# One transformer layer on one core: FFN's first weight block by halves of the tokens in the passage, a later copy in the shift, dot products in other heads, new operand offsets

## The chip, the cores and the metric

The kernel runs on one core of a Trainium2 chip. The metric is the device time of one execution in microseconds (us). A profile of one execution is read with it; its times count from the start of its span.

## The reference

One layer of a diffusion transformer for 256 latent tokens and 256 context tokens, width D = 2048, all in fp32:

```python
h = modulate(rms_norm(x, g_attn_pre), sh1, sc1)          # latent tokens
hc = modulate(rms_norm(ctx, g_attn_pre), csh1, csc1)     # context tokens
# window attention (8 heads, 2 key heads, rotary, sinks) and
# neighbourhood attention (8 heads, position bias), both with the context as further keys
y = (sigmoid(ga) * (oa @ w_br_a) + sigmoid(gb) * (ob @ w_br_b)) @ w_o
x = x + gt1 * rms_norm(y, g_attn_post)
h = modulate(rms_norm(x, g_ffn_pre), sh2, sc2)
a, g = split(depthwise_conv(h @ w_up, conv_w, conv_b))   # conv over tokens, width 3
x = x + gt2 * rms_norm((silu(g) * a) @ w_down, g_ffn_post)
```

The six modulation vectors come from `silu(c) @ w_mod + b_mod`. `w_up` is 2048 x 11264, `w_down` 5632 x 2048.

## The kernel before

Every fp32 product is made of fp32r matmuls on TensorE (PE): each operand is split into a high part (ScalarE, ACT, copies it as fp32r) and a low part (VectorE, DVE, subtracts). `split` at L123 does both; L127 is ACT's copy, L131 DVE's subtraction. A product is high x high, high x low and low x high. In `mm2` the first two are one matmul of 512 columns (the moving operand holds the high and low parts of 256 tokens side by side) and the third is one of 256 columns.

Weights come as blocks of 128 x 2048 in the order of use: `raw_block` loads one over SyncE's DMA queue (SP), `halves` splits it in two pieces of 128 x 1024, `block(ahead)` hands out the next block, splits the one after it and loads `ahead` blocks further. `place` names other memory for a block's split, `queue` instructions behind which it has to stand.

The stages: keys with the modulation vectors (`dot`, `mods`), where `shift` is part of the last keys; values; 16 attention heads with the query projections as filler in between; gates and branches; W_O (`norm_gain`, matmuls `py_o`); the passage to the FFN; `w_up` in blocks (`pu`); `w_down` (`py_d`). A Tile scheduler puts each engine's instructions in order; where the program says `tc.issue_after(i)` an instruction stands behind `i`, and under `manual_schedule` PE's order is that of the code.

The parts that the change touches:

- **The passage.** `norm_gain` runs W_O in four chunks `c` of 512 output columns over two token halves `t` (128 tokens each). In the last chunk the last `lead` = 2 weight blocks are run for t = 0 first, then for t = 1, twelve matmuls a block and half, so that t = 0 is closed earlier. `close(t)` squares on ACT (`Square`, row sums in `ss`) and multiplies by the gain on DVE (`yg`); `residual(t)` (`done`) adds to the stream (`x1`, STT of DVE, L988) and takes the sums of squares of the result; `rstd_tok` gives 1/rms in `r`. For t = 1 the last 512 columns of the residual are made by PE itself (`ident` x `x1`, then the diagonal `dg` x `yg`), to save DVE's steps. The normalised result goes to FFN's layout by transposes on PE into `ptx`: `turn(b, ts)` transposes group b of 128-column tiles j; `scaled(t, c0, c1)` multiplies tiles c0 to c1 by `r` ahead of it (into `yg`); for t = 0 and the first four groups the diagonal `dg1` does that on PE. `split_h2(b)` makes high and low parts of h: ACT L1043 (with scale and shift), DVE L1047 and L1048; every fourth tile by ACT L1042 and L1043 and DVE L1045. `first_pairs(k)` runs the four output tiles `pu0..3` for tile k of the contraction. `keep_busy` runs matmuls of no use while PE would wait (L236).
- **Shift.** The last of the six vectors' products with PE (`pmsh`), copied by ACT (`evsh`, L567), and transposed back.
- **Attention.** Per head: `scores` (`s`), softmax on ACT and DVE, `transposes` (`pT`), `values` (`po`); `q_rope` rotates the queries of the window heads. Every operand lies in one tile `room` at offsets counted in T2 = 512. Four `mods` dot products on DVE stand behind heads p = 1, 4, 7, 10.

PSUM has six banks of `acc` and two of `bank`.

Of the kernel before, what the change touches and what calls it, by code (L numbers as in the profile page):

```python
# [15 lines left out]
P = 128  # L16
# [42 lines left out]
def layer_kernel(ctx, tc, xc, xt, ccol, crow, wm_sc, wm_sd, wm_sh, wm_b, cols, wk, wkt, ws, rope, mask_a, bias_b, out):  # L59
# [74 lines left out]
    def halves(r, off, pool=None, after=None):  # L134
        n = r.shape[-1]
        b = 1 if pool else 2
        h, lo = (
            (pool or wp).tile([P, 2048 + 128], F32R, tag=f"w{q}", bufs=b, name=f"w{q}{nraw[0]}")[:, off : off + 2048]
            for q in "hl")
        for q in (slice(0, n // 2), slice(n // 2, n)):  # L140
            last[:] = split(h[:, q], lo[:, q], r[:, q], after)
        return h, lo
# [98 lines left out]
    with ExitStack() as mx:  # L241
# [10 lines left out]
        with ExitStack() as at:  # L252
# [279 lines left out]
            for k in range(KT):  # L532
# [27 lines left out]
                for i in range(k % 4 == 1, NK2):  # L560
                    keys(pk[i], *units[KT + k // 2], (k % 2) * NK2 * P + i * P, k)
                    if k == KT - 2 and i < 2:
# [4 lines left out]
                        nc.scalar.activation(ev[:, :n_], pm[:, 2 * P * i : 2 * P * i + n_], AF.Copy)  # L567
# [122 lines left out]
            def q_split(hd, t):  # L690
                o = 4 * T2 + order.index(hd) % 3 * T2
# [42 lines left out]
            def keys_of(hd):  # L734
                i = NHB + hd // GRP if hd < NHA else hd - NHA
                if i not in ks:
                    o = [(len(ks) % 2 * 2 + q) * T2 for q in range(2)]
                    ks[i] = [room[:, q : q + T2] for q in o]
                    split(*ks[i], kT[:, i], last)
                return ks[i]  # L740

            def vals_of(hd):
                i = hd // GRP if hd < NHA else 2 + hd - NHA
                if i not in vs:

                    o = [(12 + len(vs) % 2 * 2 + q) * T2 - 8 for q in range(2)]
# [32 lines left out]
            def transposes(hd):  # L779
                pT = pTs[hd] = room[:, 7 * T2 : 11 * T2].rearrange("p (b a s) -> p b a s", b=4, a=2)  # L780
# [25 lines left out]
            for p in range(NH + 1):  # L806
# [14 lines left out]
                if p in (1, 4, 7, 10):  # L821
# [48 lines left out]
    def norm_gain(act, nk, yg, grow, ss, nm, lead, done, extra=None):  # L870


        for c in range(4):
            py = [acc(f"py_{nm}{c}_{t}") for t in range(2)]
# [13 lines left out]
            def close(t, after=None):  # L888
                with ExitStack() as es:
                    if after:  # L890
                        es.enter_context(tc.issue_after(after))
                    nc.scalar.activation(yg[:, t, cs], py[t][:], AF.Square, accum_out=ss[:, t, c : c + 1])
                nc.vector.tensor_tensor(out=yg[:, t, cs], in0=py[t][:], in1=grow[:, cs], op=ALU.mult)
# [13 lines left out]
            else:  # L907
# [4 lines left out]
                for t in range(2):  # L912
                    if t:
                        for i, g in enumerate(range(n - lead, n)):
                            part(wts[i], g, 1)
                    close(t, after)
                    after = done(t)
# [14 lines left out]
    with ExitStack() as ys:  # L932
# [20 lines left out]
        crb = silu_row(yp)  # L953
        gain_row(0, grow)
        place[b0 + B_UP - 1] = yp

        pu, dg = [], {}

        def diagonal(n, t):

            dg[n] = yp.tile([P, P], F32, name=f"dg{n}")
            return nc.scalar.activation(dg[n][:], ident[:], AF.Copy, scale=r[:, n, t : t + 1]).ins
# [7 lines left out]

        def residual(t):
            rstd_tok(ss[:, 0, t], r[:, 0, t : t + 1])
            c3 = slice(1536, 2048)
            if t:

                pu.extend(acc(f"pu0_{i}") for i in range(4))
                px = pu[3]
                with tc.issue_after(final[0]):
                    p_ = nc.tensor.matmul(px[:], ident[:], x1[:, t, c3], start=True, stop=False).ins
                with tc.issue_after(p_):  # L980
                    b_ = keep_busy(4, "2", pu[0])
                with tc.issue_after(diagonal(0, t)):
                    diagonal(1, 0)
                with tc.issue_after(b_):
                    p_ = nc.tensor.matmul(px[:], dg[0][:], yg[:, t, c3], start=False, stop=True).ins
            for c in range(3 if t else 4):
# [5 lines left out]
                if t and c == 2:  # L992
# [9 lines left out]
            if t == 0:  # L1002
                rstd_tok(ss[:, 1, t], r[:, 1, t : t + 1])
                return a_.ins
            with tc.issue_after(v_.ins), tc.issue_after(a_.ins):
                return p_, rstd_tok(ss[:, 1, t], r[:, 1, t : t + 1])[0]

        p_, q_ = norm_gain(zz, KT, yg, grow, ss[:, 0], "o", 2, residual, beside)
        zs.close()


        group = [(0,)] + [(j, j + 1) for j in range(1, KT - 1, 2)] + [(KT - 1,)]
        ptx, behind = {}, []

        def turn(b, ts, js=None):

            if b not in ptx:
                ptx[b] = (acc if b % 2 else bank)(f"ptx{b}")
            for t in ts:
                for f, j in enumerate(group[b]):  # L1020
                    if js and j not in js:
                        continue
                    d = ptx[b][:, f * S + t * P : f * S + t * P + P]
                    if t == 0 and b < 4:
                        nc.tensor.matmul(d, x1[:, t, j * P : j * P + P], dg[1][:], start=True, stop=True)
                    else:
                        nc.tensor.transpose(d, yg[:, t, j * P : j * P + P], ident[:])

        def split_h2(b):
            with ExitStack() as es:  # L1030
                for i_ in behind:
                    es.enter_context(tc.issue_after(i_))
                behind[:] = split_tiles(b)
            return behind

        def split_tiles(b):
            for f, j in enumerate(group[b]):
                g_, s_ = gcol[:, 1, j : j + 1], modx[:, 16 + j : 17 + j]
                px = ptx[b][:, f * S : f * S + S]
                t_ = up.tile([P, S], F32, tag="half", bufs=2, name=f"h2t{j}")  # L1040
                if j % 4 == 3:
# [273 lines left out]
```

## Time and profile before

| | |
|---|---|
| median of 3 runs | 1512.99 us (1512.9 to 1513.67) |
| the profiled execution | 1512.95 us, span 1511.0 us |
| PE busy | 1499.6 us, 99% |
| DVE busy | 1132.4 us, 75% |
| ACT busy | 781.6 us, 52% |
| TensorE clock granted | 0.999 |

A row of the trace in order of time has start and duration in us, the engine, the line of the code, the operation, `out<-in` with shapes, and in brackets the idle time of the engine ahead of it and what ended that. `x4` joins four instructions. A plain fp32 matmul leaves two records. "PE A <- B" in a list of waits is time in which PE stood for B: total, times, longest. Of the chain that ended last, PE has 97%.

### The profile page before, as it was taken

What the parts mean: (1) busy time and instruction counts of PE and PEld (TensorE: products, weight loads), DVE (VectorE), ACT (ScalarE), POOL (GpSimd) and SP (SyncE); (2) the same over time, 40 slices, a digit from 0 to 9 for tenths busy, and PEclk for the clock granted to TensorE, in tenths of its full rate; (3) what the DMA queues carried; (4) which work ended last, traced back from release to release, by engine and by line L of the source; (5) the groups of instructions that cost most, each with busy time, mean ns of one, the idle gap of its engine ahead of it and who ended that gap; (6) DMA issues with size and microseconds to landing.
All of it is one profiled execution on the core that took longest, in us unless ns stands there. A gap on an engine that the chain in (4) does not pass through costs nothing.

```text
span 1511.0 us, 21644 instructions
## 1 busy us (share of the span) xinstructions
PE 1499.6 (99%) x8549; PEld 1289.3 (85%) x8549; DVE 1132.4 (75%) x1679; ACT 781.6 (52%) x1277; POOL 1.6 (0%) x10
## 2 busy tenths in 40 slices
PE   9999999999999999999999999999999999999998
PEld 7876889898888888888888888888888888888886
DVE  4496997999988888877678888788788776444444
ACT  4342542777764455554467555555555555344342
POOL 0000000000000000000000000000000000000000
PEclk9999999999999999999999999999999999999999
DMA  9988779754368888879846676666666556555552
GB/s 368 401 319 335 273 290 341 263 168 168 140 252 294 324 327 308 309 268 356 309 178 226 249 250 220 238 243 236 234 248 232 192 192 257 217 195 195 195 195 84
DMA packets 59253, 381.07 MB, mean 252 GB/s; under 512 B 6544, under 2 KB 6928, under 8 KB 17040
## 3 DMA queue, kind: packets, MB, share of 16 engines
q1 hardware_dynamic: 58432, 378.63, 67.5%
q8 instruction: 67, 1.10, 0.3%
q10 hardware_dynamic: 720, 1.07, 0.2%
q14 instruction: 34, 0.28, 0.1%
HBM read 375.43 MB, written 4.24 MB: 251 GB/s over the span
## 4 chain that ended last, share of the span: by engine, by line
PE 97%; DVE 1%; DMA 1%; ACT 1%; issue 0%; DVEq 0%; ACTq 0%
PE pu L174 21%; PE py_d L883 16%; PE pu L175 11%; PE pv L656 7%; PE pg L174 7%; PE pk L438 7%; PE py_o L883 6%; PE pq L174 4%; PE pb L174 4%; PE pg L175 4%; PE pq L175 2%; PE pb L175 2%; PE s L763 1%; PE po L793 1%; PE pm L312 1%; PE pt L784 1%
## 5 line engine op out<-in xcount | busy, mean ns | idle before, releaser
L131 DVE TENSOR_TENSOR wl<-raw,wh 128x1024 fp32r<-128x1024 f32 x444 | 529.9, 1221 | 222.8 <-ACT wh L127 222.7
L127 ACT ACTIVATE wh<-raw 128x1024 fp32r<-128x1024 f32 x444 | 452.9, 1054 | 294.6 <-PE py_d L883 129.2
L174 PE MATMUL pu<-h,wh 128*128 128x512 f32 x1404 | 488.1, 391 | 0.0
L175 PE MATMUL pu<-h,wl 128*128 128x256 f32 x1404 | 395.9, 282 | 0.0
L174 PEld LDWEIGHTS pu<-h,wh 128*128 128x128 f32 x1404 | 263.6, 188 | 55.6 <-issue 0.4
L175 PEld LDWEIGHTS pu<-h,wl 128*128 128x128 f32 x1404 | 265.4, 189 | 0.0
L883 PE MATMUL py_d<-wh,ff 128*128 128x512 f32 x704 | 216.8, 389 | 0.0
L174 PE MATMUL pg<-h,wh 128*128 128x512 f32 x464 | 161.5, 390 | 0.0
L883 PEld LDWEIGHTS py_d<-wh,ff 128*128 128x128 f32 x704 | 132.1, 188 | 27.6
L204 DVE SCALAR_TENSOR_TENSOR raw<-raw,crb 128x2048 f32<-128x2048 f32 x64 | 146.2, 2285 | 8.8 <-DMA raw<-in_wm_b_dram 8.7
L883 PE MATMUL py_d<-wl,ff 128*128 128x512 f32 x352 | 136.9, 389 | 0.0
L175 PE MATMUL pg<-h,wl 128*128 128x256 f32 x464 | 130.8, 282 | 0.0
L438 PE MATMUL pk<-h,ku 128*128 128x512 f32 x480 | 118.1, 398 | 0.9 <-DVE ku L131 0.4
L179 ACT ACTIVATE half_u<-pu 128x256 f32<-128x256 f32 x88 | 33.5, 383 | 152.7 <-PE pu L175 152.7
L438 PEld LDWEIGHTS pk<-h,ku 128*128 128x128 f32 x480 | 87.5, 188 | 25.6 <-issue 4.8
L174 PE MATMUL pq<-h,wh 128*128 128x512 f32 x304 | 108.6, 395 | 0.0
L174 PEld LDWEIGHTS pg<-h,wh 128*128 128x128 f32 x464 | 87.1, 188 | 18.2
L656 PE MATMUL pv<-wh,h 128*128 128x512 f32 (+1 forms) x384 | 101.8, 354 | 0.0
L174 PE MATMUL pb<-h,wh 128*128 128x512 f32 x256 | 89.4, 390 | 0.0
L175 PEld LDWEIGHTS pg<-h,wl 128*128 128x128 f32 x464 | 87.7, 189 | 0.0
L175 PE MATMUL pq<-h,wl 128*128 128x256 f32 x304 | 85.5, 281 | 0.0
L180 DVE TENSOR_TENSOR u<-pu,half_u 128x256 f32<-128x256 f32 x88 | 37.1, 423 | 56.7 <-ACT half_u L179 56.6
(193 smaller groups left out, 1790.4 us busy)
## 6 DMA issues: line engine op xcount, KB each, us to landing
raw<-in_ws_dram SPq DMA_DIRECT2D x222, 1024.0 KB, 4.8
raw<-in_wm_b_dram SPq DMA_DIRECT2D x64, 1024.0 KB, 4.9
raw<-in_wm_sc_dram SPq DMA_DIRECT2D x15, 1024.0 KB, 7.4
raw<-in_wm_sh_dram SPq DMA_DIRECT2D x16, 768.0 KB, 6.8
raw<-in_wkt_dram SPq DMA_DIRECT2D x10, 1024.0 KB, 5.1
raw<-in_wk_dram SPq DMA_DIRECT2D x7, 768.0 KB, 8.0
crb<-sild SPq DMA_DIRECT2D x5, 1024.0 KB, 6.4
sd<-in_wm_sd_dram SPq DMA_DIRECT2D x4, 1024.0 KB, 8.1
```

What stands on the lines that cost most here:

```text
L127: a_ = nc.scalar.activation(hi, src, AF.Copy)
L131: v_ = nc.vector.tensor_tensor(out=lo, in0=src, in1=hi, op=ALU.subtract)
L174: nc.tensor.matmul(pt[:, :], wh[:, w], a, start=first and i == 0, stop=False, skip_group_check=True)
L175: nc.tensor.matmul(pt[:, :S], wl[:, w], a[:, 0], start=False, stop=last and i == n - 1, skip_group_check=True)
L179: a_ = nc.scalar.activation(t[:], pt[:, S:], AF.Copy)
L180: v_ = nc.vector.tensor_tensor(out=out_, in0=pt[:, :S], in1=t[:], op=ALU.add)
L204: nc.vector.scalar_tensor_tensor(out=r, in0=r, scalar=1.0, in1=row, op0=ALU.mult, op1=ALU.mult, accum_out=modx[:, j : j + 1])
L312: nc.tensor.matmul(pm[32 * j : 32 * j + 32, t * P : t * P + P], cc[:, q, :], rsc[k + t][:, q * P : q * P + P], start=q < 4, stop=q >= KT - ...
L438: nc.tensor.matmul(pk[:], wt[:, w], hh[:, :, k, a], start=k == 0 and a == 0 and wt is wh, stop=k == KT - 1 and a == 1)
L656: nc.tensor.matmul(pv[i][:, :nw], src[:, k, a, t0 : t0 + P], wt[:, w], start=k == 0 and q == 0, stop=k == KT - 1 and q == 2)
L763: nc.tensor.matmul(s_ps[:], qs[hd][:, a, qt * P : qt * P + P], k_, start=q == 0, stop=q == 2)
L883: p_ = nc.tensor.matmul(py[t][:], act[:, k, a, t * P : t * P + P], wt[:, w], start=k == 0 and q == 0, stop=k == nk - 1 and q == 2)
```

## The change

- `norm_gain` gets lead 3 and a hook `ahead`. `ahead(0)`, after the t = 0 matmuls, takes the `pu` banks and splits the first half of FFN's second weight block into `crt`, the memory that `crb` used to hold. `ahead(1)` is called inside W_O's very last part, after three of its twelve matmuls: it transposes tiles j = 0 to 3 of t = 0 (groups "a" and "b"), splits them to h in halves of 128 tokens, and scales tiles 4 to 7. `close(1)` is queued behind that.
- `half_pairs(k, t)` runs tile k for one token half: per output tile a matmul of 2 x 128 columns and one of 128 columns. For t = 0 tiles 0 to 3 run before t = 1 is normalised, around the `dg` matmul and in place of most of the filler; for t = 1 they follow as t = 1's tiles arrive (k = 0 in twelve matmuls of 128 columns). The `dg1` matmuls are gone. `px` gets its own bank.
- Groups are now "a" (0, 1), "b" (2, 3) for t = 0; 0: (0), 1: (1, 2, 3) for t = 1; and 2 to 7: (4, 5) to (14, 15) for both. `scaled` for tiles 8 to 11 and 12 to 15 is placed later, behind the weight split of FFN's second block and the tiles ahead of it. Two W_O blocks, not one, are split to other memory (`tail`, `yp`).
- The last square of `residual(0)` runs on DVE.
- Shift: the `evsh` copies stand behind the last key split.
- Attention: `mods` behind heads 1, 3, 5, 7; offsets of queries, keys, `pT` and values in `room` moved; the last two blocks of values use 16 instead of 8.

```diff
-                parts[q] = halves(raws[q], 8 if q - b0 < B_Q else 0, place.get(q), queue.get(q))
+                parts[q] = halves(
+                    raws[q], 8 if q - b0 < B_Q - 2 else 16 if q - b0 < B_Q else 0, place.get(q), queue.get(q), int(q == b0 + B_UP + 1))
...
-                        nc.scalar.activation(ev[:, :n_], pm[:, 2 * P * i : 2 * P * i + n_], AF.Copy)
+                        with tc.issue_after(done_u[KT + KT // 2 - 1][0]):
+                            nc.scalar.activation(ev[:, :n_], pm[:, 2 * P * i : 2 * P * i + n_], AF.Copy)
...
-                o = 4 * T2 + order.index(hd) % 3 * T2
+                o = order.index(hd) % 3 * T2
...
-                    o = [(len(ks) % 2 * 2 + q) * T2 for q in range(2)]
+                    o = [3 * T2 + 8 + (len(ks) % 2 * 2 + q) * T2 for q in range(2)]
...
-                if p in (1, 4, 7, 10):
+                if p in (1, 3, 5, 7):
...
-            def part(wts, g, t):
+            def part(wts, g, t, between=None):
                 wh, wl = wts
                 for kk in range(4):
+                    if between and kk == 1:
+                        between()
...
+                if ahead:
+                    ahead(0)
...
-                            part(wts[i], g, 1)
+                                part(wts[i], g, 1, (lambda: before.extend(ahead(1))) if ahead and i == lead - 1 else None)
...
+        def half_pairs(k, t, part=0):
+            ts = slice(t * P, t * P + P)
+            wh, wl = parts[nb_[0]]
+            for i in range(4):
+                w = slice(k % 4 * 512 + i * P, k % 4 * 512 + i * P + P)
+                both = pu[i][:].rearrange("p (a s) -> p a s", a=2)[:, :, ts]
+                if part == 0:
+                    nc.tensor.matmul(
+                        both, wh[:, w], h2[:, k, :, ts], start=k == 0 and t == 0, stop=False, skip_group_check=True)
+                    nc.tensor.matmul(pu[i][:, ts], wl[:, w], h2[:, k, 0, ts], start=False, stop=False, skip_group_check=True)
...
+                half_pairs(0, 0)
+                half_pairs(1, 0)
+                p_ = nc.tensor.matmul(px[:], dg[0][:], yg[:, t, c3], start=False, stop=True).ins
...
-                if t and c == 2:
+                if c == (2 if t else 3):
...
+        def ahead(i):
+            if i == 0:
+                nb_[0] = nblk[0]
+                pu.extend(acc(f"pu0_{i}") for i in range(4))
+                r_ = raws[nb_[0] + 1]
+                with tc.issue_after(last[0]), tc.issue_after(last[1]):
+                    split(crt[:, : D // 2], crt[:, D // 2 :], r_[:, : D // 2])
+            else:
+                for b in "ab":
+                    turn(b, (0,))
+                for j in range(4):
+                    split_h2("ab"[j // 2], t0, (j,))
+                scaled(0, 4, 8)
+                return behind[:]
...
-        p_, q_ = norm_gain(zz, KT, yg, grow, ss[:, 0], "o", 2, residual, beside)
+        p_, q_, px = norm_gain(zz, KT, yg, grow, ss[:, 0], "o", 3, residual, beside, ahead)
...
+            half_pairs(2, 0)
+            half_pairs(3, 0)
+            for b in (2, 3):
                 turn(b, (0,))
-            keep_busy(8, "3", pu[0])
+            keep_busy(3, "3", ptx[0])
...
+            half_pairs(0, 1, 1)
+            split_h2(1, t1, (1,))
+            half_pairs(0, 1, 2)
+            split_h2(1, t1, (2, 3))
+            half_pairs(1, 1)
             turn(2, (1,))
+            split_h2(2)
+            half_pairs(2, 1)
+            turn(3, (1,))
+            queue[nblk[0] + 1] = behind[:]
             block(3)
             behind[:] = last
+            with tc.issue_after(behind[0]):
+                behind[0] = scaled(0, 8, 12, True)
+            half_pairs(3, 1)
             split_h2(3)
+            with tc.issue_after(behind[1]):
+                behind[1] = scaled(1, 8, 12)
...
-                b = {5: 4, 7: 5, 8: 6, 10: 7, 12: 8}.get(k)
+                b = {5: 4, 7: 5, 9: 6, 11: 7}.get(k)
...
+                if k in (5, 9, 12):
+                    queue[nblk[0] + 1] = behind[:]
+                    block(3)
+                    behind[:] = last
```

What the change moves, at three places. First PE at the end of W_O. Before, its last matmul is followed by the identity product, filler, the `dg` product, the diagonal transposes of t = 0 (`dg_7065` is the second diagonal), and filler again (`py_o_1` is t = 1's bank, `zz` the branch result):

```order
L883 MATMUL py_o_1_6901<-wl_6967,zz 128x512
L979 MATMUL pu_3_7057<-x_6466,ident 128x512
L236 MATMUL pu_0_7054<-ident 128x128 x4
L985 MATMUL pu_3_7057<-yg,dg_7063 128x512
L1025 MATMUL ptx_7082<-dg_7065,x_6466 128x128
L1025 MATMUL ptx_7084<-dg_7065,x_6466 128x128 x2
L1025 MATMUL ptx_7087<-dg_7065,x_6466 128x128 x2
L1025 MATMUL ptx_7090<-dg_7065,x_6466 128x128 x2
L236 MATMUL pu_0_7054<-ident 128x128 x8
L1027 MATMUL ptx_7082<-ident,yg 128x128
```

Now, in the midst of the last part (its block is `wh_6952`, `wl_6953`):

```order
L891 MATMUL py_o_1_6901<-wh_6952,zz 128x512 x2
L891 MATMUL py_o_1_6901<-wl_6953,zz 128x512
L1054 MATMUL ptxa<-ident,yg 128x128 x2
L1054 MATMUL ptxb<-ident,yg 128x128 x2
L891 MATMUL py_o_1_6901<-wh_6952,zz 128x512 x2
```

and after the half products of t = 0 and the transposes of tiles 4 to 7, ahead of the half products of t = 1:

```order
L996 MATMUL pu_3_6995<-h_6462,wl_6973 128x128
L1054 MATMUL ptx_7136<-ident,yg 128x128 x2
L1054 MATMUL ptx_7139<-ident,yg 128x128 x2
L241 MATMUL ptx_7142<-ident 128x128 x3
L1054 MATMUL ptx_7142<-ident,yg 128x128
L1054 MATMUL ptx_7155<-ident,yg 128x128 x3
L999 MATMUL pu_0_6992<-h_6462,wh_6972 128x128
L999 MATMUL pu_0_6992<-h_6462,wl_6973 128x128
```

The transposes of tiles 0 to 3 of t = 0 have moved from behind W_O into its last part, and the diagonal matmuls and most of the filler are gone.

Second DVE around the closing of t = 1, before (`x_6466` is the residual stream):

```order
L988 SCALAR_TENSOR_TENSOR x_6466<-yg,r,x_6466 128x512 x4
L922 TENSOR_REDUCE r<-ss 128x1
L923 TENSOR_SCALAR r<-r 128x1
L925 RECIPROCAL r<-r 128x1
L893 TENSOR_TENSOR yg<-py_o_1_6901,grow 128x512
L925 RECIPROCAL r<-r 128x1
L988 SCALAR_TENSOR_TENSOR x_6466<-yg,r,x_6466 128x512 x3
```

and now (`h_6462` is h in high and low parts, `ptxa` and `ptxb` the transposed halves):

```order
L983 TENSOR_SCALAR yg<-x_6466,r 128x512 x2
L1070 TENSOR_SCALAR h2t_0_7052<-h_6462,modx 128x128
L1071 SCALAR_TENSOR_TENSOR h_6462<-ptxa,gcol,h2t_0_7052 128x128
L1070 TENSOR_SCALAR h2t_0_7056<-h_6462,modx 128x128
L1071 SCALAR_TENSOR_TENSOR h_6462<-ptxa,gcol,h2t_0_7056 128x128
L1070 TENSOR_SCALAR h2t_0_7060<-h_6462,modx 128x128
L1071 SCALAR_TENSOR_TENSOR h_6462<-ptxb,gcol,h2t_0_7060 128x128
L1070 TENSOR_SCALAR h2t_0_7064<-h_6462,modx 128x128
L1071 SCALAR_TENSOR_TENSOR h_6462<-ptxb,gcol,h2t_0_7064 128x128
L901 TENSOR_TENSOR yg<-py_o_1_6901,grow 128x512
L938 RECIPROCAL r<-r 128x1
L1020 SCALAR_TENSOR_TENSOR x_6466<-yg,r,x_6466 128x512 x3
```

The eight instructions of the t = 0 halves, and two scalings, now stand between the residual of t = 0 and the product `yg<-py_o_1`. On ACT, `Square` of `py_o_1` stands behind the four `h<-ptxa`, `h<-ptxb` in the same way.

Third the scaling of tiles 8 to 11 of t = 1 on DVE, before (the last of the `yg<-x` rows), ahead of every tile of h:

```order
L925 RECIPROCAL r<-r 128x1
L969 TENSOR_SCALAR yg<-x_6466,r 128x128
L969 TENSOR_SCALAR yg<-x_6466,r 128x384
L969 TENSOR_SCALAR yg<-x_6466,r 128x512 x2
L1047 TENSOR_SCALAR h2t_7109<-h_6462,modx 128x256
L1048 SCALAR_TENSOR_TENSOR h_6462<-ptx_7082,gcol,h2t_7109 128x256
```

and now (`ptx_7136` holds tiles 4 and 5, `ptx_7139` 6 and 7; the last row is that scaling):

```order
L1070 TENSOR_SCALAR h2t_0_7193<-h_6462,modx 128x256
L1071 SCALAR_TENSOR_TENSOR h_6462<-ptx_7136,gcol,h2t_0_7193 128x256
L1070 TENSOR_SCALAR h2t_0_7197<-h_6462,modx 128x256
L1071 SCALAR_TENSOR_TENSOR h_6462<-ptx_7136,gcol,h2t_0_7197 128x256
L131 TENSOR_TENSOR wl_7212<-raw_6958,wh_7211 128x1024
L1070 TENSOR_SCALAR h2t_0_7226<-h_6462,modx 128x256
L1071 SCALAR_TENSOR_TENSOR h_6462<-ptx_7139,gcol,h2t_0_7226 128x256
L1068 TENSOR_TENSOR h_6462<-h2t_0_7230,h_6462 128x256
L983 TENSOR_SCALAR yg<-x_6466,r 128x512
```

It has moved behind tiles 0 to 7 and half a weight block. PE takes it up here, in the transposes of tiles 8 and 9 (`ptx_7244`), between k = 4 and k = 5:

```order
L180 MATMUL pu_2_6994<-h_6462,crt 128x256
L179 MATMUL pu_3_6995<-h_6462,crt 128x512
L180 MATMUL pu_3_6995<-h_6462,crt 128x256
L1054 MATMUL ptx_7244<-ident,yg 128x128 x4
L179 MATMUL pu_0_6992<-h_6462,crt 128x512
L180 MATMUL pu_0_6992<-h_6462,crt 128x256
```

where before the transposes at that place were those of tiles 7 and 8 (`ptx_7197`):

```order
L175 MATMUL pu_2_7056<-h_6462,wl_7146 128x256
L174 MATMUL pu_3_7057<-h_6462,wh_7145 128x512
L175 MATMUL pu_3_7057<-h_6462,wl_7146 128x256
L1027 MATMUL ptx_7197<-ident,yg 128x128 x4
L174 MATMUL pu_0_7054<-h_6462,wh_7145 128x512
L175 MATMUL pu_0_7054<-h_6462,wl_7146 128x256
```

so what PE needs there comes now from a scaling that stands after tile 7 on DVE.

More of the change, by code (lines that the diff above doesn't have):

```diff
@@ L132, in split, with halves @@
         return a_.ins, v_.ins
-    def halves(r, off, pool=None, after=None):
+    def halves(r, off, pool=None, after=None, first=0):
         n = r.shape[-1]
         b = 1 if pool else 2
[L137 to L140, printed above, removed]
+        if isinstance(pool, tuple):
+            h, lo = pool
+        else:
+            h, lo = (
+                (pool or wp).tile([P, 2048 + 128], F32R, tag=f"w{q}", bufs=b, name=f"w{q}{nraw[0]}")[:, off : off + 2048]
+                for q in "hl")
+        for q in (slice(0, n // 2), slice(n // 2, n))[first:]:
             last[:] = split(h[:, q], lo[:, q], r[:, q], after)
@@ L974, in residual @@
             if t:
[L976 to L985, printed above, removed]
+                px = acc("px")
+                nc.tensor.matmul(px[:], ident[:], x1[:, t, c3], start=True, stop=False)
+                dg[0] = yp.tile([P, P], F32, name="dg0")
+                nc.scalar.activation(dg[0][:], ident[:], AF.Copy, scale=r[:, 0, t : t + 1])
+                half_pairs(0, 0)
+                half_pairs(1, 0)
+                p_ = nc.tensor.matmul(px[:], dg[0][:], yg[:, t, c3], start=False, stop=True).ins
             for c in range(3 if t else 4):
@@ L1013, in layer_kernel, with turn @@
+        group = {"a": (0, 1), "b": (2, 3), 0: (0,), 1: (1, 2, 3)}
+        group.update({2 + i: (4 + 2 * i, 5 + 2 * i) for i in range(6)})
         ptx, behind = {}, []
-        def turn(b, ts, js=None):
+        def turn(b, ts):
             if b not in ptx:
-                ptx[b] = (acc if b % 2 else bank)(f"ptx{b}")
+                ptx[b] = (acc if b in (2, 3, 5, 7) else bank)(f"ptx{b}")
+            n = S if b in range(2, 8) else P
             for t in ts:
                 for f, j in enumerate(group[b]):
[L1021 to L1027, printed above, removed]
@@ L1029, in split_h2, with split_tiles @@
-        def split_h2(b):
+                    o = f * n + (t * P if n == S else 0)
+                    nc.tensor.transpose(ptx[b][:, o : o + P], yg[:, t, j * P : j * P + P], ident[:])
+        def split_tiles(b, ts=slice(0, S), js=None):
+            n = ts.stop - ts.start
+            for f, j in enumerate(group[b]):
+                if js and j not in js:
+                    continue
+                g_, s_ = gcol[:, 1, j : j + 1], modx[:, 16 + j : 17 + j]
+                px = ptx[b][:, f * n : f * n + n]
+                t_ = up.tile([P, S], F32, tag="half", bufs=2, name=f"h2t{j}_{ts.start}")[:, :n]
+                if j % 4 == 3 and n == S:
+                    nc.scalar.activation(t_, px, AF.Identity, scale=g_, bias=s_)
+                a_ = nc.scalar.activation(h2[:, j, 0, ts], px, AF.Identity, scale=g_, bias=s_)
+                if j % 4 == 3 and n == S:
+                    v_ = nc.vector.tensor_tensor(out=h2[:, j, 1, ts], in0=t_, in1=h2[:, j, 0, ts], op=ALU.subtract)
+                else:
+                    nc.vector.tensor_scalar(out=t_, in0=h2[:, j, 0, ts], scalar1=s_, scalar2=None, op0=ALU.subtract)
+                    v_ = nc.vector.scalar_tensor_tensor(
+                        out=h2[:, j, 1, ts], in0=px, scalar=g_, in1=t_, op0=ALU.mult, op1=ALU.subtract)
+            return a_.ins, v_.ins
@@ L1030, in split_h2 @@
+        def split_h2(b, *args):
             with ExitStack() as es:
@@ L1032, in split_h2 @@
                     es.enter_context(tc.issue_after(i_))
[L1033 removed]
+                behind[:] = split_tiles(b, *args)
             return behind
[L1036 to L1041, printed above, removed]
[L1042 to L1050 removed]
@@ L1053, in first_pairs @@
[L1053 to L1063 removed]
+        nb_ = [0]
```

101 lines of the change are left out of this document (44 added, 57 removed).

## The prediction

> **What bounds the kernel now.** I read the page's first lines, then the list of what PE waited for, then PE's, ACT's and DVE's rows in order of time around the four places that the change touches. The page's head, its engine line and its clock line:
>
> ```profile
> span 1511.0 us, 21644 instructions
> PE 1499.6 (99%) x8549; PEld 1289.3 (85%) x8549; DVE 1132.4 (75%) x1679; ACT 781.6 (52%) x1277; POOL 1.6 (0%) x10
> PEclk9999999999999999999999999999999999999999
> ```
>
> PE is busy all the way at an undiminished clock. Time falls only if PE gets less work or less waiting, and any new wait of PE costs its full length. The list of waits, PE's own:
>
> ```profile
> PE pu L1061 <- ACT h L1043: 0.4, 1, 0.4
> PE pk L438 <- DVE ku L131: 0.4, 1, 0.4
> PE s L763 <- ACT h L127: 0.2, 1, 0.2
> ```
>
> At the places of the change that is all there is to remove, 1.0 us, beside 0.26 for `dg` in a row below. What else is removable is filler that PE runs while it would wait. In the passage from W_O to the first FFN block that is:
>
> ```profile
> 764.99 0.39 PE L883 MATMUL py_o<-wl,zz 128*128 128x512 f32 x1
> 765.22 1.02 PE L979 MATMUL pu<-x,ident 128*128 128x512 f32 x2
> 766.08 1.05 PE L236 MATMUL pu<-ident 128*128 128x128 f32 x8
> 767.39 1.12 PE L985 MATMUL pu<-yg,dg 128*128 128x512 f32 x2 [0.26 <-ACT dg L962]
> 768.35 1.72 PE L1025 MATMUL ptx<-dg,x 128*128 128x128 f32 x14
> 769.91 1.95 PE L236 MATMUL pu<-ident 128*128 128x128 f32 x16
> 771.70 0.49 PE L1027 MATMUL ptx<-ident,yg 128*128 128x128 f32 x3
> 772.86 0.28 PE L1061 MATMUL pu<-h,wl 128*128 128x256 f32 x1
> 773.55 0.28 PE L1061 MATMUL pu<-h,wl 128*128 128x256 f32 x1
> 780.29 0.60 PE L1027 MATMUL ptx<-ident,yg 128*128 128x128 f32 x4
> ```
>
> W_O's matmuls start 0.23 apart (0.227 unrounded) and end at 765.22; FFN work starts at 772.6 (the last wait for `h` in the list); the L236 rows (2.8 us) are pure filler, the x14 row is diagonal matmuls that plain transposes replace. A plain fp32 matmul of 128 columns leaves two records, so the x16 row is 8 in 1.95 us less its tail, 0.22 each; seven fp32r matmuls of 256 columns start within 0.69 us, 0.115 each; a transpose of 128 columns takes 0.11 (0.49 less a last one's 0.27, by two).
>
> **The passage, step by step.** ACT and DVE set it. Their rows:
>
> ```profile
> 759.98 0.60 ACT L892 ACTIVATE yg<-py_o 128x512 f32<-128x512 f32 x1 [3.65 <-PE py_o L883]
> 761.50 2.74 DVE L988 SCALAR_TENSOR_TENSOR x<-yg,r,x 128x512 f32<-128x512 f32 x4
> 765.42 0.60 ACT L892 ACTIVATE yg<-py_o 128x512 f32<-128x512 f32 x1
> 769.04 0.69 DVE L994 SCALAR_TENSOR_TENSOR yg<-x 128x512 f32<-128x512 f32 x1
> 770.85 1.41 DVE L969 TENSOR_SCALAR yg<-x,r 128x128 f32<-128x128 f32 x4
> 772.01 1.02 ACT L1043 ACTIVATE h<-ptx,modx,gcol 128x256 fp32r<-128x256 f32 x2 [0.49 <-PE ptx L1027]
> 773.47 0.34 DVE L1047 TENSOR_SCALAR h2t<-h,modx 128x256 f32<-128x256 f32 x1
> 773.91 0.48 DVE L1048 SCALAR_TENSOR_TENSOR h<-ptx,gcol,h2t 128x256 fp32r<-128x256 f32 x1
> 774.43 0.56 ACT L1043 ACTIVATE h<-ptx,modx,gcol 128x256 fp32r<-128x256 f32 x1 [1.40 <-DVE h L1048]
> 777.34 2.36 DVE L131 TENSOR_TENSOR wl<-raw,wh 128x1024 fp32r<-128x1024 f32 x2
> 780.60 0.56 ACT L1043 ACTIVATE h<-ptx,modx,gcol 128x256 fp32r<-128x256 f32 x1 [1.88 <-DVE h L1048]
> 782.71 0.43 DVE L1045 TENSOR_TENSOR h<-h2t,h 128x256 fp32r<-128x256 f32 x1 [0.25 <-ACT h L1043]
> ```
>
> The row at 774.43 matters most: ACT reads the second tile of a PSUM bank only 0.04 us after DVE has read the first (773.91 + 0.48). So tiles of one bank go in series: ACT 0.56, DVE 0.35 and 0.48. For tiles half as wide I estimate 0.46, 0.29 and 0.35, with two hand-overs about 1.25 us a tile.
>
> (1) W_O's last chunk is closed for t=0 after lead 3 instead of 2: twelve more matmuls, 12 x 0.227 = 2.72 us, so the Square moves from 759.98 to 757.3. The four STT of the residual come 1.52 us later as before and end at 761.6. The last square now runs on DVE; from there to the scaled values takes 1.81 us (769.04 to 770.85), and the first slice of 512 another 0.48: 763.8.
>
> (2) PE has 27 of the 36 t=1 matmuls ahead of the four inserted transposes: 757.05 + 27 x 0.227 = 763.2. It waits 0.7 us there, runs 0.44 of transposes and 0.09 of changing back. W_O ends at 766.45, +1.2 (0.5 if the slice is in time, 1.5 with the 0.2 spread of these steps).
>
> (3) The four t=0 halves of h, two to a bank, occupy ACT from 764.2 to 767.75. The Square of `py_o_1` is queued behind them, so it starts at 767.75 instead of 766.7: 2.3 us later than in the row at 765.42.
>
> (4) From that Square to the first t=1 transpose took 6.28 us (771.70). Half products of k = 0 to 3 replace the filler; 6.1 is left by the same chain, since only three filler matmuls stand in front: 773.8, +2.1.
>
> (5) From there PE has 0.8 us to the first pair, 12 matmuls of 128 columns (1.3 + 0.1), three half pairs of 1.0, two pairs of transposes (0.44), and one full k (4 x 0.345 = 1.4): it reaches the transposes of tiles 8 and 9 at about 781.0.
>
> (6) These need yg(0,8,12) (ACT) and yg(1,8,12) (DVE). In the row at 770.85 the latter is the last of the four; now it stands on DVE behind tiles 0 to 3 of t=1, 4 and 5, the second half of a weight block, and 6 and 7. From 773.8: first tile 1.5, the other three, all in one bank, to 778.55 (0.65, 1.25, 1.25); tile 4 0.9; tile 5, whose ACT read waits for tile 4, 1.6; the weight half 1.2; tile 6 0.9; tile 7, two ACT operations and the 0.43 subtraction, 1.6; the slice 0.5. That is 785.2. PE waits 0.7 for ACT's slice and 3.4 more for DVE's: 4.0 us that are nowhere in the list above.
>
> (7) k = 5 then starts at 785.4 instead of 780.7 (after the row at 780.29). Twelve transposes instead of fourteen remain (-0.2); the block for k = 12, whose DVE half is now behind tiles 12 and 13, comes 0.75 late by the same durations. The passage costs +5.1 us; from +1.1 if the wait of (6) is gone, to +6.5 if each ACT and DVE step is 0.1 longer.
>
> The weight splits that move ahead of this (W_O's three last blocks every 2.7 us instead of 5.45, half an FFN block into `crt`, their loads on SP with them) I cost at nothing: a block takes DVE 2.36 (row at 777.34), and ACT idles 3.65 us before the row at 759.98. Without that cover PE would wait up to 1.2 us, half a block on DVE, once.
>
> What has no row is an fp32r matmul of 128 columns, of which there are 40. Bounds: 0.058, half of 256 columns; 0.22, a plain fp32 one of that shape. I take 0.11, the transposes, because that is the row with the same shape and one weight load each. At 0.058 the end would move by -0.4, at 0.22 by +2.65: the first sixteen give 1.3 (1.8 less 0.45 that PE waits for `dg` anyway), and the ones in front of the transposes of tiles 4 to 7 another 1.3, which the chain of (6) hands on. The Trainium skill ("TensorE: Matmul & The Clock Gate", "Back-to-back issue gap") gives about 81 ns for a sustained stream at 128 columns; by it the sum would be 0.2 us lower, an estimate, and no run here shows it.
>
> **Shift.** ACT's order and the stall it makes:
>
> ```profile
> 144.47 0.55 ACT L567 ACTIVATE evsh<-pmsh 128x256 f32<-128x256 f32 x2 [7.47 <-PE pmsh L542]
> 144.91 1.07 ACT L127 ACTIVATE ku<-ru 128x1024 fp32r<-128x1024 f32 x1
> 146.01 1.23 DVE L131 TENSOR_TENSOR ku<-ru,ku 128x1024 fp32r<-128x1024 f32 x1 [8.48 <-ACT ku L127]
> 147.29 0.73 PE L438 MATMUL pk<-h,ku 128*128 128x512 f32 x2 [0.39 <-DVE ku L131]
> ```
>
> ACT sat 7.5 us behind `evsh` with the key split queued behind it. Split first, ku is ready some microseconds early and the stall goes: -0.5 (0.39 and the tail of the pipeline refilling). The two copies still start at 144.5, when PE delivers. Ends: 0, if `ru` lands late, and -0.6.
>
> **Attention.** Only one head's start shows a wait:
>
> ```profile
> 369.44 2.29 DVE L204 SCALAR_TENSOR_TENSOR raw<-raw,crb 128x2048 f32<-128x2048 f32 x1
> 372.15 0.28 PE L793 MATMUL po<-h 128*128 128x256 f32 x1
> 372.64 0.73 PE L763 MATMUL s<-h 128*128 128x512 f32 x2 [0.22 <-ACT h L127]
> ```
>
> The last two rows start 0.49 apart where 0.12 is due: 0.37 lost after a 2.29 us dot product held DVE up in a rotated head. Moved dot products take that away: -0.3; ends -0.5, and +0.4 if it returns in an unrotated head.
>
> **Alignment.** Groups by shape over the attention stage, `s` and `po` beside `pq`, whose operands stay where they were:
>
> ```profile
> L174 PE MATMUL pq<-h,wh 128*128 128x512 f32 x304 | 108.6, 395 | 0.0
> L175 PE MATMUL pq<-h,wl 128*128 128x256 f32 x304 | 85.5, 281 | 0.0
> L793 PE MATMUL po<-h 128*128 128x256 f32 x189 | 26.5, 281 | 0.0
> L763 PE MATMUL s<-h 128*128 128x512 f32 x96 | 26.0, 395 | 0.2 <-ACT h L127 0.2
> ```
>
> Equal means, so little to win: -0.2; ends 0 and -0.6 (6 ns, the distance from 395 to the 389 of `py_d` in the page, on 96).
>
> **Sum.** +5.1 - 0.5 - 0.3 - 0.2 = +4.1. The profiled execution took 1512.95 us (its span and 1.95 around it; the median of the runs is 1512.99, the same): 1517.0 us.
>
> **Rivals.** First, the 40 matmuls of 128 columns go at the pace of plain fp32: 1519.7. For it: no fp32r matmul in the whole trace is under 256 columns, so no row excludes it. Against: records of plain fp32 come in twos, and these need not.
>
> Second, the other side: yg(1,8,12) is in time. Place: the transposes of tiles 8 and 9. DVE's work in front of it is 7.3 us if it runs without a gap, which ends at 781.9, 0.5 to 0.9 after PE arrives; from there PE waits hardly longer than for ACT. It decides at the series through a bank: if tiles of one bank overlap, the wait falls by 3.3 us and the late block of k = 12 by 0.75, which leaves the passage at +1.0 against the small parts' -1.0: 1513.0, no change, and 1512.3 if the 0.7 at the inserted transposes goes too. Against it stand the gaps of 1.40 and 1.88 in ACT's rows.
>
> Third, PE's clock after the wait. The start of the trace:
>
> ```profile
> 1.94 3.36 PE L236 MATMUL busy<-ident 128*128 128x128 f32 x14 [1.94 <-POOL ident masks.py:199]
> ```
>
> Fourteen records take 3.36 us there, 0.24 each; sixteen later take 1.95, 0.12 each. After a pause PE can run at half pace for 3.4 us, though the granted clock in the records reads full. If the 3.4 us at tile 8 are pause enough, 14 x 0.12 = 1.7 us come on top: 1518.7. No pause of that length stands inside the trace of before (0.4 at most). The Trainium skill ("TensorE: Matmul & The Clock Gate", "The HAM clock gate") says that an idle window of about 3.4 us halves the clock until about as long a busy one has passed; by that rule the sum is 1518.7 as well, right at its edge, and the trace's start agrees with the half pace.
>
> Fourth, the slice is in time and the new offsets are worth 10 ns on each of the 285 matmuls of `s` and `po`, which no row shows or excludes: a passage of 0.0, then -0.5, -0.3 and -2.85, 1509.3.
>
> **How the numbers follow.** Forecast 0.36 (its own range 1515.5 to 1518.5), plain fp32 pace 0.22, slice in time 0.20, slow clock 0.08, larger gain from the offsets 0.14. About 0.2%, 3.0 us, is what a measurement of this kernel tells from no change: faster is under 1510.0, slower over 1516.0. Slower: three quarters of the forecast (0.27), all of the first and third rival: 0.57. Same: the rest of the forecast and the second: 0.29. Faster: the fourth, 0.14. The range goes from 1511.5 (the slice in time, small parts at their ends) to 1520.2 (plain fp32 pace and 0.5), which leaves out about 2 in 10.
>
> **What would show it.** In the trace after: PE waiting for DVE yg right before the transposes of tiles 8 and 9, 3 to 4 us, the largest wait of PE; 0.7 ahead of the four transposes inside W_O; the second Square at 767 to 768; the spacing of the 128-column matmuls, 0.11 or 0.22; no wait of pk for ku at 147; `s` 0.12 after `po`. I am wrong if the first of these is under 1 us, or if PE's work in the passage shrinks by more than the 2.8 us of filler.

## The result, and the profile after

| | before | changed |
|---|---|---|
| median of 6 runs | 1512.91 us (1512.76 to 1513.67) | 1518.65 us (1517.68 to 1519.75) |
| the profiled execution | 1512.95, span 1511.0 | 1519.75, span 1518.0 |
| clock granted to PE | 0.999 | 0.996 |

The ratio is 1.0038, interval 1.0025 to 1.005: slower by 5.7 us, 1.65 us over the forecast of 1517.0, inside the whole range given (1511.5 to 1520.2) and 0.15 outside the forecast's own (1515.5 to 1518.5). The profiled execution of the changed kernel is the slowest of its six, and its sums are made against its own time.

PE's waits in the changed kernel at the places of the change (total us, times, longest):

```profile
PE ptx L1054 <- DVE yg L983: 3.0, 1, 3.0
PE s L769 <- DVE h L131: 0.8, 1, 0.8
PE px L1017 <- ACT dg L1014: 0.6, 1, 0.6
PE ptx L1054 <- ACT yg L982: 0.4, 1, 0.4
PE ptxa L1054 <- DVE yg L983: 0.2, 1, 0.2
```

The first is the wait of step (6). The waits of pk for ku and of s for ACT, 0.4 and 0.2 before, are gone, but s waits for DVE in another place. PE's rows around the transposes of tiles 8 and 9:

```profile
781.23 0.44 PE L1054 MATMUL ptx<-ident,yg 128*128 128x128 f32 x2 [0.37 <-ACT yg L982]
784.64 0.69 PE L1054 MATMUL ptx<-ident,yg 128*128 128x128 f32 x2 [2.98 <-DVE yg L983]
784.98 0.78 PE L179 MATMUL pu<-h,crt 128*128 128x512 f32 x1
785.55 0.42 PE L180 MATMUL pu<-h,crt 128*128 128x256 f32 x1
785.77 0.63 PE L179 MATMUL pu<-h,crt 128*128 128x512 f32 x1
```

After the wait a matmul of 256 columns starts 0.21 us ahead of the next, and one of 512 columns 0.43: half pace. The granted clock of the same stretch, in the row by stages (PE, PEld, DVE, ACT, POOL busy, then PEclk):

```profile
781.60:783.50 1.90, 0.07 (x1) 0.00 (x0) 0.97 (x3) 0.82 (x3) 0.00 (x0) 1.00 0.31 43
783.50:784.00 0.50, 0.00 (x0) 0.00 (x0) 0.24 (x1) 0.50 (x2) 0.00 (x0) 0.60 0.71 246
784.00:790.30 6.30, 5.66 (x19) 4.89 (x20) 4.15 (x9) 3.36 (x5) 0.00 (x0) 0.50 0.32 134
790.30:791.00 0.70, 0.70 (x6) 0.67 (x5) 0.70 (x1) 0.03 (x1) 0.00 (x0) 0.91 0.00 0
```

The clock was cut at about 783.6, about 2 us after PE's last work, the transpose that ends at 781.67, and came back at about 790.4. The products of k = 5 and 6, from the first of them to the next group's first transpose, took 5.3 us.

What made the slice late, on ACT and DVE:

```profile
765.59 0.46 ACT L1066 ACTIVATE h<-ptxa,modx,gcol 128x128 fp32r<-128x128 f32 x1 [0.81 <-DVE h L1071]
767.79 0.59 ACT L900 ACTIVATE yg<-py_o 128x512 f32<-128x512 f32 x1
775.80 0.46 ACT L1066 ACTIVATE h<-ptx,modx,gcol 128x128 fp32r<-128x128 f32 x1 [0.91 <-DVE h L1071]
779.05 0.56 ACT L1066 ACTIVATE h<-ptx,modx,gcol 128x256 fp32r<-128x256 f32 x1 [1.14 <-DVE h L1071]
782.71 0.56 ACT L1065 ACTIVATE h2t<-ptx,modx,gcol 128x256 f32<-128x256 f32 x1 [1.08 <-DVE h L1071]
784.11 0.48 DVE L983 TENSOR_SCALAR yg<-x,r 128x512 f32<-128x512 f32 x1
```

The second Square (L900) starts at 767.79 and the slice (L983) is made at 784.11 to 784.59; ahead of the Square and between the two, ACT stops where it comes to the next tile of a bank that DVE is reading.

By the start of PE's last matmul of each group (changed against before): keys -0.84, values -1.46, attention +0.11, W_O +1.17, the FFN's end +6.17. The rest, 0.8 of the span's 7.0, lies behind PE's last matmul, which ends 7.4 us before the span's end in the kernel before and 8.2 in the changed one.

### The profile page after: what moved, and what is told of

It is laid out like the page before. It is cut to its first block, busy times and chain, and to the rows that moved or that the text cites. A ratio compares the mean times of both kernels' runs of the same rounds, so it can differ in the third digit from the quotient of the medians.

```text
span 1518.0 us, 21667 instructions
## 1 busy us (share of the span) xinstructions
PE 1501.9 (99%) x8556; PEld 1291.7 (85%) x8556; DVE 1136.3 (75%) x1692; ACT 781.8 (52%) x1276; POOL 1.6 (0%) x10
## 4 chain that ended last, share of the span: by engine, by line
PE 89%; DVE 5%; DMA 3%; issue 1%; ACT 1%; SPq 0%; DVEq 0%; ACTq 0%
PE pu L179 21%; PE py_d L891 16%; PE pu L180 11%; PE pk L443 7%; PE pg L179 7%; PE py_o L891 5%; PE pq L179 4%; PE pb L179 4%; PE pg L180 4%; PE pb L180 2%; PE pq L180 2%; DMA raw<-in_wm_b_dram 2%; PE po L799 2%; PE s L769 1%; DVE wl L131 1%
## 5 line engine op out<-in xcount | busy, mean ns | idle before, releaser
L179 PE MATMUL pu<-h,wh 128*128 128x512 f32 x1384 | 481.4, 391 | 0.0
L180 PE MATMUL pu<-h,wl 128*128 128x256 f32 x1384 | 391.3, 283 | 0.0
L179 PEld LDWEIGHTS pu<-h,wh 128*128 128x128 f32 x1384 | 260.5, 188 | 54.0
L209 DVE SCALAR_TENSOR_TENSOR raw<-raw,crb 128x2048 f32<-128x2048 f32 x58 | 132.5, 2286 | 11.7 <-DMA raw<-in_wm_b_dram 11.2
```

The source lines that it names most:

```text
L179: nc.tensor.matmul(pt[:, :], wh[:, w], a, start=first and i == 0, stop=False, skip_group_check=True)
L180: nc.tensor.matmul(pt[:, :S], wl[:, w], a[:, 0], start=False, stop=last and i == n - 1, skip_group_check=True)
L209: nc.vector.scalar_tensor_tensor(out=r, in0=r, scalar=1.0, in1=row, op0=ALU.mult, op1=ALU.mult, accum_out=modx[:, j : j + 1])
```

## The experiments

Every median stands beside runs of the kernel before on the same chip: 1513.33 us (27 runs) for the first four; 1513.22 (22) for the passage alone, ACT first in a group and one dot product fewer; 1513.42 (21) for ACT first alone and the kernel before with ACT first; 1513.05 (21) for the last two.

**The slices early.** In `ahead(1)` and after q:

```diff
                 scaled(0, 4, 8)
+                scaled(0, 8, 12)
...
-            behind[:] = [q_, scaled(1, 4, 8)]
+            scaled(1, 4, 8)
+            behind[:] = [q_, scaled(1, 8, 12)]
...
-            with tc.issue_after(behind[0]):
-                behind[0] = scaled(0, 8, 12, True)
...
-            with tc.issue_after(behind[1]):
-                behind[1] = scaled(1, 8, 12)
```

> The changed kernel with the two scaled slices of tiles 8 to 11 made where DVE idles: t=0 right after tiles 4 to 7 of t=0, t=1 right after tiles 4 to 7 of t=1. Theory A (PE's wait at tiles 8 and 9, 0.37 + 2.98 us, and a half-pace clock that this pause brings, about 2.5 us between 785 and 790.7): both go, 1518.65 - 5.9 = 1512.8 us, and the matmuls of k = 5 are 0.23 and 0.12 apart. Rival B (the slow pace has another cause, such as operands in crt or traffic of DVE and ACT): only the wait goes, 1515.3, and k = 5 and 6 stay slow. Rival C (the series of tiles on ACT and DVE is the limit anyhow): the wait moves to the next transposes or products, 1516 or more.

Measured 1516.81, ratio 1.0025 (1.0015 to 1.0034). The wait at tiles 8 and 9 and the slow clock are gone (clock 0.999), but PE now waits later:

```profile
PE pu L180 <- DVE wl L131: 1.6, 2, 1.0
PE pu L179 <- ACT wh L127: 1.1, 1, 1.1
```

They are for the splits of FFN's third weight block (1.1 and 1.0 us at k = 8) and of its fourth (0.6 at k = 12). Between W_O's first matmul and the FFN's end the kernel lost 3.6 us against before; the changed kernel lost 6.1. So theory A was right on the cause, but its 1512.8 is 4.0 us too low. The time is rival C's (1516 or more): 2.7 us of waits are new.

**Filler in the wait.** Ahead of the transposes of tiles 8 and 9:

```diff
                 if b:
+                    if b == 4:
+                        ptx[4] = bank("ptx4")
+                        keep_busy(14, "4", ptx[4])
                     turn(b, (0, 1))
```

> The changed kernel with 14 matmuls of no use (0.22 us each, 3.1 us) on PE just ahead of the transposes of tiles 8 and 9, in the time in which it waits. Theory A: the wait for the slice stays (the transposes at the same moment), PE is never idle for long, so k = 5 and 6 run at full pace and the time falls by 2.5 us to 1516.1; the clock shown is 0.999. Rival B: the pace of k = 5 and 6 stays, 1518.6.

Measured 1517.26, ratio 1.0031 (1.002 to 1.0042). PE's rows, and the clock behind them:

```profile
779.53 3.29 PE L241 MATMUL ptx<-ident 128*128 128x128 f32 x28
783.46 0.44 PE L1054 MATMUL ptx<-ident,yg 128*128 128x128 f32 x2 [0.42 <-DVE yg L983]
783.65 0.48 PE L179 MATMUL pu<-h,crt 128*128 128x512 f32 x1
783.97 0.28 PE L180 MATMUL pu<-h,crt 128*128 128x256 f32 x1
```

```profile
783.60:786.60 3.00, 3.00 (x19) 2.66 (x19) 1.29 (x4) 1.65 (x3) 0.00 (x0) 1.00 0.40 167
```

The transposes come as late as in the changed kernel (18.46 us after W_O's last matmul starts, there 18.47), yet the clock is full and k = 5 and 6 take 2.9 us instead of 5.3. So it is the pause that brings the slow pace, not the operands or the traffic, and rival B falls. Net it is worth 1.7 us between W_O's first matmul and the FFN's end, not 2.5: that stretch loses 4.4 instead of 6.1, as the weights of k = 12 are then waited for (0.6), which the slow pace had hidden.

**All parts but the passage.** Before with the hunks of the shift, the offsets and the heads.

> The kernel before with all parts but the passage: copies behind the key split, dot products behind heads 1, 3, 5, 7, all new offsets. Theory D (shift gives 0.65 and the values' offset 0.62, but the first heads wait for weight blocks whose loads are late, as the loads are the limit there): 1513.0 us, with PE waiting for DVE h at the second head. Rival E (the loss at the second head in the changed kernel was that execution's alone): 1511.5.

Measured 1512.93, ratio 0.9997 (0.9989 to 1.0006): no change, though PE's last matmul in the profiled execution is 1.0 us earlier than before. The time is D's, but not for D's reason: this execution has no stop at the second head, and loses 0.8 behind PE's last matmul (8.2 us to the end, not 7.4).

**Shift and value offset alone.**

> The kernel before with the copies behind the key split and the last value blocks at offset 16 only; the dot products behind heads 1, 4, 7, 10 and attention's offsets as before. Theory D: the gain of 1.3 us is lost at the first heads here as well, 1512.9. Rival F (the loss comes from the other heads' dot products or the offsets in attention): 1511.6.

Measured 1513.41 (1511.58 to 1515.39), ratio 0.9999 (0.9991 to 1.0008). The runs fall in two groups: five from 1511.58 to 1511.91, six from 1513.41 to 1515.39. The profile shows one of the second:

```profile
PE s L764 <- DVE h L131: 0.8, 1, 0.8
```

Here is why, in DVE's rows of this execution and then of the one with all small parts, which did not lose:

```profile
262.74 2.29 DVE L204 SCALAR_TENSOR_TENSOR raw<-raw,crb 128x2048 f32<-128x2048 f32 x1 [3.16 <-DMA raw<-in_wm_b_dram]
```

```profile
260.29 2.29 DVE L204 SCALAR_TENSOR_TENSOR raw<-raw,crb 128x2048 f32<-128x2048 f32 x1 [0.40 <-DMA raw<-in_wm_b_dram]
```

A dot product of the value stage waits 3.16 us for its load in one and 0.40 in the other. Its slot is the one into which the next weight block is loaded; ACT then splits that block at 272.86 after waiting 1.95 for it (270.22 and 0.79 in the other), and DVE's key split of the second head comes late. Neither D nor F is right alone: in these two traces the landing of a load goes with whether the gain of 1.0 to 1.5 us is kept. That the two groups of runs differ by it is likely and not shown, since only one execution of this kernel was traced. Nor does the late load need the two parts: the trace of the passage alone, where shift and values are as before, has it too,

```profile
263.11 2.29 DVE L209 SCALAR_TENSOR_TENSOR raw<-raw,crb 128x2048 f32<-128x2048 f32 x1 [3.34 <-DMA raw<-in_wm_b_dram]
```

and PE stops for 0.73 at its second head.

**The passage alone.** The changed kernel with the small parts undone.

> The kernel before with the change of the passage alone; the shift, the dot products and all offsets as before. If the parts add: the changed kernel's 1518.65, less what the small parts bring, which is between 0.0 (their gain lost at the second head, as in the changed kernel's trace) and 1.4: 1518.7 to 1520.0, with the wait of 3.4 us at tiles 8 and 9 and the slow k = 5 and 6. If the small parts hurt: under 1518.3.

Measured 1518.41, ratio 1.0032 (1.0019 to 1.0044), with the same wait of 2.98 and half pace. That is 0.3 under what adding up the parts gave. The passage is the whole loss; the small parts brought nothing measurable.

**ACT first in a group.** The kernel with early slices, and `split_tiles` in two loops, first ACT's operations of all tiles of the group, then DVE's; the t = 0 halves now go through it a bank at a time, so that the order holds for them as well:

```diff
+            todo = []
             for f, j in enumerate(group[b]):
...
                 a_ = nc.scalar.activation(h2[:, j, 0, ts], px, AF.Identity, scale=g_, bias=s_)
+                todo.append((j, g_, s_, px, t_))
+            for j, g_, s_, px, t_ in todo:
                 if j % 4 == 3 and n == S:
...
-                for j in range(4):
-                    split_h2("ab"[j // 2], t0, (j,))
+                for b in "ab":
+                    split_h2(b, t0)
...
```

> As the kernel with the early slices, and in each group of tiles ACT's operations of all its tiles now stand ahead of DVE's, so that ACT's read of the second tile no longer waits for DVE's read of the first in the same PSUM bank. Theory C (what the passage lacks is time on ACT and DVE, most of it this series): PE's waits for the weight split at k = 8 (2.5 us there) and at k = 12 (1.0) shrink by 2 us together, 1514.8. Rival G (the limit is DVE's work itself, 27 us of 33 in the passage): PE's waits stay within 0.5 us of what they were, 1516.5.

Measured 1511.19, ratio 0.9987 (0.9979 to 0.9996): faster than the kernel before and than the one with early slices, and 3.6 us under theory C's 1514.8. In the passage PE's waits are down to two:

```profile
PE pu L999 <- ACT h L1067: 0.2, 1, 0.2
PE ptxa L1054 <- DVE yg L983: 0.2, 1, 0.2
```

ACT's rows show pairs without a stop for DVE, where the changed kernel had one at each second tile; one stop is left, 1.04 us between tiles 1 and 2:

```profile
776.14 1.02 ACT L1067 ACTIVATE h<-ptx,modx,gcol 128x256 fp32r<-128x256 f32 x2 [0.69 <-PE ptx L1054]
777.06 1.06 ACT L127 ACTIVATE wh<-raw 128x1024 fp32r<-128x1024 f32 x1
```

From W_O's first matmul to the FFN's end it is 1.2 us shorter than before. Theory C expected 2 us of waits to go; 2.7 went, and with the earlier closing of t = 1 the FFN's end comes 4.8 us sooner after W_O's first matmul than with early slices alone.

**ACT first alone**, with the slices as late as in the changed kernel.

> The changed kernel with ACT's operations of a group ahead of DVE's, and the slices of tiles 8 to 11 late as they are in it. Theory C (the series through a bank is what makes the slice late): four steps of about 0.9 us fall out ahead of the slice, PE's wait at tiles 8 and 9 drops to 0.5 to 1 us, the clock stays full, and the time is within 0.7 of the kernel with both edits: 1511.2 to 1512. Rival L (the place of the slice is what counts): PE still waits 2 us or more there, 1514.

Measured 1513.62, ratio 1.0002 (0.9993 to 1.0011). The wait is 1.6 us, between what C and L gave; the clock does not fall:

```profile
780.86 0.44 PE L1054 MATMUL ptx<-ident,yg 128*128 128x128 f32 x2 [1.56 <-DVE yg L983]
```

```profile
781.00:784.00 3.00, 3.00 (x19) 2.68 (x19) 1.89 (x6) 2.66 (x4) 0.00 (x0) 1.00 0.72 306
```

So the series made about half of the wait of 3.35, and the slice's place the other half; counted from W_O's first matmul, this wait ends 2.8 us sooner than in the changed kernel. The time is 1.6 over the top of C's span: W_O to FFN takes 1.8 longer than with both edits, which is about the wait. Against the kernel before this execution also loses 0.5 at the second head and 1.1 behind PE's last matmul.

**The kernel before with ACT first.**

> The kernel before with ACT's operations of a group ahead of DVE's. ACT's waits for DVE in the passage (7.1 us in four) go; PE hardly waits for h there, so the time stays: 1513.1, within 0.2%.

Measured 1512.61, ratio 0.9993 (0.9984 to 1.0002): no change that can be told. ACT's waits cost the kernel before little, at most 0.5 us between W_O's first matmul and the FFN's end by the traces.

**One dot product fewer in the value stage**, heads 1, 2, 4, 5, 7, with shift and value offset.

> The kernel before with the copies behind the key split, the value offset 16, one dot product fewer in the last value block, and dot products behind heads 1, 2, 4, 5, 7, all unrotated; attention's offsets as before. Theory D (the second head waits for a weight block that SP can load only when a dot product's slot is free, and that dot product waits for its own load): the loss at the second head is gone in every execution, 0.65 + 0.62 + 0.3 gained, 1511.5 with runs close together. Rival H (the loads there are late whatever the dot products do): runs in two groups as with the two parts alone, 1511.6 and 1513.4 or more.

Measured 1512.80 (1512.49 to 1513.69), ratio 0.9998 (0.9989 to 1.0007). The runs no longer stand in two groups and the second head hardly loses (0.3), as D had it, and PE's last matmul starts 0.93 earlier than before. But the 1511.5 expected did not come: 8.9 us lie behind that matmul's end instead of 7.4. The writes of the result take longer to land. Their groups after PE's last matmul, in the kernel before and then in this one (KB each, us to landing):

```profile
out_dram<-x1b ACTq DMA_DIRECT2D x2, 256.0 KB, 2.0
out_dram<-x1b SPq DMA_DIRECT2D x2, 256.0 KB, 2.1
```

```profile
out_dram<-x1b ACTq DMA_DIRECT2D x2, 256.0 KB, 2.7
out_dram<-x1b SPq DMA_DIRECT2D x2, 256.0 KB, 2.9
```

By the traffic of the same view the extra time is a trickle: here the rate falls from 308 GB/s to 9 to 27 for the last 1.6 us, in the kernel before it falls from 293 to nothing.

**Heads alone, and the best version.** Before with heads 1, 3, 5, 7 and nothing else; and the kernel with ACT first, with heads 1, 4, 7, 10 and attention's offsets as before.

> The kernel before with the dot products behind heads 1, 3, 5, 7 and nothing else. Theory J: the stop of 0.37 at the rotated head goes, two of 0.22 come, and the end after the last matmul is 8.0 or more instead of 7.4: 1513.2 + 0.8 = 1514.0. Rival K: 7.4, and 1513.2.

> The kernel with ACT's operations first, with the dot products behind heads 1, 4, 7, 10 and attention's offsets as in the kernel before (the copies behind the key split and the value offset stay). Theory J: the moved dot products lengthen the time from PE's last matmul to the end (8.0 to 8.9 us in the six traces that have them, 7.3 to 7.4 in the three that have not), and attention's new offsets make an s matmul 2 ns slower: 7.4 again, 1511.19 - 0.8 - 0.2 = 1510.2, with the 0.37 at a rotated head back in place of two of 0.22. Rival K (the landing of the last write varies by chance): within 0.3 of 1511.2.

Heads alone: 1513.83, ratio 1.0003 (0.9994 to 1.0012), with 8.2 us behind the last matmul: 0.8 slower by the medians, which the interval can't tell from nothing, with the profiled end as J said. PE's stop of 0.37 at the rotated head went and one of 0.25 came. The best version: 1510.53 (1510.25 to 1513.78), ratio 0.9986 (0.9977 to 0.9995), 7.4 us behind the last matmul; J gave 1510.2, K 1511.2. Its lead over the kernel with ACT first is not shown: that one's ratio to the kernel before is 0.9987, with nearly the same interval. In all eight traces with moved dot products that end is 8.0 to 8.9 us, in the five without 7.3 to 7.6. Why the place of a dot product at 290 to 420 us should change how fast the last writes land was not found, and stays open.

## Why the prediction was right

Step (1) and (2): the Square of t = 0 came at 757.49, the inserted transposes waited 0.2 and not 0.7, and W_O lost 1.06 of the 1.2 given. PE reached the transposes 0.5 later than I had it, 0.1 of which was there when W_O began.

Steps (3) and (4): the Square of t = 1 at 767.79 (767.75 given), the first t = 1 transpose of tile 0 at 773.64 (773.8).

Step (5): the 128-column matmuls of k = 0 start 0.11 apart, as taken from the transposes, so the first rival is out. In a half pair the 256-column matmul is followed after 0.17 and the 128-column one after 0.06, 0.23 together, which is what 0.115 + 0.11 gave.

PE was ready for the transposes of tiles 8 and 9 at 780.86; the terms of step (5) add to 780.84, though 781.0 was written.

Step (6): PE waited 0.37 + 2.98 us, 3.35 of the 4.0 given, as the slice ended at 784.59 and not 785.2. The mechanism, tiles in series through a PSUM bank and the slice behind them, is shown by the two runs with ACT first; that it was a matter of the slice's place as well, by the run that moved only that.

Step (7): the late block of k = 12 did not show in the changed kernel, because the slow clock gave it time; it is there (0.6) once the clock is full, and in the run with early slices the blocks of k = 8 and 12 are where the wait went. The terms of this step add to 5.2, not 5.1, and the four tiles of step (6) to 778.45, not 778.55; neither moves the forecast by more than 0.1.

The third rival was not the alternative to the forecast but a part of what happened, on top of it. It was priced at 1.7 us and given a chance of 0.08; filler in the wait shows 1.7 net. I held a pause of 3.4 us to be right at the edge. Two traces have the slow clock, the changed kernel's and that of the passage alone: it fell 1.9 and 1.6 us after PE's last work and was low for 6.8 us in both, while the pause of 1.56 us in the run with ACT first alone left it full. So a pause under 3.4 us can be enough. How long one may be these traces do not say: counted from the last transpose, 1.6 us was cut and 1.56 was not; counted from the last fp32r product ahead of the transposes, the clock fell after 2.7 and 2.4 us, and 2.0 us without a product left it full. The Trainium skill ("TensorE: Matmul & The Clock Gate", "The HAM clock gate") has about 3.4 us for each; the half clock agrees (0.50 in the row), the low time is twice that figure, and the fall came sooner than it.

So the median, 1518.65, is the third rival's 1518.7 and not the forecast's 1517.0, and that too is partly luck, since two further errors nearly cancel. The passage without the slow clock cost 4.4 (the run with filler), not 5.1; and the small parts, forecast at -1.0, gave nothing that can be measured (the passage alone 1518.41, all but the passage 1512.93).

The small terms were wrong singly, and their sum of -1.0 shows only in the place of PE's last matmul in the run with all of them; the longer end behind it took back 0.8. Shift gave 0.65 (0.5 forecast). The offsets gave 0.62, but in the values, at a place that I had not looked at: the 256-column matmuls of the value stage, before and changed, over 242 to 261 us of each:

```profile
L656 PE MATMUL pv<-wh,h 128*128 128x256 f32 x107 | 19.4, 283 | 0.0
```

```profile
L662 PE MATMUL pv<-wh,h 128*128 128x256 f32 x110 | 19.3, 279 | 0.0
```

Their spacing went from 120 to 116.7 ns, 3.3 ns on 192 matmuls. In attention itself the new offsets made s no faster: six s matmuls in a row take 1.56 us where they took 1.54 or 1.55, some 2 ns each. (The group's mean, 397 against 395, holds the stop at the second head too, and is 397 in the run with shift and value offset, whose attention offsets are those of before.) The moved dot products brought 0.1 at best and the longer end. And what the second head lost where a load was late, up to 1.8 us, no step had: I had priced a key split that is ready earlier as a gain, and not asked when the loads behind it land.

## What to carry to other kernels

When work of a chain that PE waits for is moved later to free an early slot, add up what now stands ahead of it on its engine, with the hand-overs, and compare that with the moment PE asks; here 0.48 us of scaling placed behind eight tiles and half a weight block cost a wait of 3.35 us and, through the clock, 1.7 more. Where PE waits for the result, let one engine finish all its reads of a PSUM bank before the other starts (where PE hardly waits, as in the kernel before, it brought nothing measurable), and try filler on PE in a pause of some microseconds that can't be avoided. Before counting on a gain ahead of a stage that waits for its loads, look in several traces at when those loads land.

## What the runs showed of the hardware that I had not expected

- The clock granted to PE fell to 0.50 in two traces, 1.9 and 1.6 us after PE's last work, and stayed there 6.8 us in both, more than 5 of them with PE busy; a pause of 1.56 us in a third did not cut it.
- Operands 32 bytes further on (offset 16 against 8 elements) made a 256-column fp32r matmul 3.3 ns faster, while attention's new offsets made 512-column ones about 2 ns slower.
- One 1 MB load was waited for 0.40 us in one trace and 3.16 in another, at the same place of kernels that are alike up to there. The runs of the second kernel stood in two groups about 2 us apart; that this load divides them is not shown.
- The last 256 KB writes took 2.0 to 2.1 us to land in kernels with the dot products in their old places and 2.3 to 2.9 in those with moved ones, whose end is the same code; the cause is open.
